# Cached cross-attention keys loaded one head at a time through two small rings, half of them during the two projections ahead of the scores

## The chip, the cores and the metric

One NeuronCore of a Trainium2 chip runs the whole program. The metric is the device time of one execution in microseconds (us), the median over runs. TensorE (PE in the profile) multiplies matrices, VectorE (DVE), ScalarE (ACT) and GpSimd (POOL) work on elements, and SyncE (SP) issues most of the transfers; 16 DMA engines carry them between the chip's memory and the on-chip buffer.

## The reference, cut to what matters

One decoder layer is computed for 256 prompt tokens and for 8 sample sequences of 4 tokens (32 sample tokens), in float32. The part that matters here is the cross-attention: the prompt tokens attend to keys and values computed from `mem_prompt`, the sample tokens to keys and values that come ready from a cache of 8 batches x 256 memory tokens x 4 heads x 512.

```python
def cross_attn(h, k, v, w_q, w_o):
    q = (h @ w_q).reshape(B, S, X_HEADS, X_HEAD_DIM)
    s = jnp.einsum('bqhd,bkhd->bhqk', q, k) * (X_HEAD_DIM ** -0.5)
    pr = jax.nn.softmax(s, axis=-1)
    o = jnp.einsum('bhqk,bkhd->bqhd', pr, v).reshape(B, S, D_MODEL)
    return o @ w_o

x = x + merged @ w_out
mk, mv = mem_kv(mem_prompt, g_mem, w_xk, w_xv)      # prompt: two more products
x = x + cross_attn(rms_norm(x, g_xattn), mk, mv, w_xq, w_xo)            # prompt
x = x + cross_attn(rms_norm(x, g_xattn), cache_mem_k, cache_mem_v, w_xq, w_xo)  # sample
```

## The kernel before, in words

All activations are held transposed (features on the 128 partitions, 288 tokens in a row). Each weight matrix is streamed in chunks of 512 rows x 512 columns (1 MB), in an order written out in `plan` (lines 121 to 143). A chunk passes through three stages: `load_w` (line 149) issues its load on SP into one of three `raw` buffers; `split_w` (line 160) makes of each half a rounded part `w_hi` on ACT (line 172) and a remainder `w_lo` on DVE (line 173), in three buffers each; `product` (lines 239 to 241) or `proj_mem` (lines 274 to 276) multiplies with three matmuls for each pair of tiles. `advance(i)` keeps the loads about three chunks and the splits two halves ahead of the half that PE is at.

Other work is put between the halves by a clock. After each half `tick()` advances it by one step (in `proj_mem` by half a step, twice a half), and runs what `later(n, fn)` put down for that step. So a step is one half of a chunk on PE. Everything is written in this order into the queue of its engine, and each engine takes its queue in order. An SP transfer that waits for a buffer therefore holds up every SP transfer behind it, the weight chunks too.

The stages around the change, one after another, have 32 steps each:

- the output projection `w_out` (in `residual`, line 828), which adds into `xT` and prepares the next operands;
- the query projection `w_xq` (loop at line 884), which writes the queries `q`. In its last quarter `mem_prompt` is loaded and transposed (lines 845 and 850);
- the memory keys `w_xk` (loop at line 1067, `proj_mem`). A quarter's result goes to memory by ACT's queue (lines 1073 and 1074). The cached keys and the sample scores are put between its steps;
- the memory values `w_xv` (loop at line 1077), with the prompt attention of one head in each quarter, and the cached values between its steps.

The cached keys of one batch are 2 MB. `k_load` (line 898) issues them as 16 transfers of 128 KB in pieces of 512 bytes, into two buffers `kv` of two heads each. `k_transposed` (line 910) transposes them on DVE, a head at a time (line 914), into `kT`, a ring of six. `k_scores` (line 920) multiplies them with `qm`, the queries of all eight batches laid out with zeros in the other batches' columns (a 128x4096 tile, cleared by POOL at line 840, filled by eight copies at line 929), and all batches are added up in one PSUM bank. A batch takes its turn every 3.8 steps of `w_xk`: load and transpose at step 1 + 3.8b, scores at 3 + 3.8b (lines 1049 to 1051). At step 31 the softmax follows (line 945), at 31.5 its transposition (line 952) with 16 DVE copies into `pTm`. The cached values come at 33 + 3.6b, a load of 1 MB and its matmuls at a time (lines 964 and 969).

Of the kernel before, what the change touches and what calls it, by code (L numbers as in the profile page):

```python
# [8 lines left out]
F32 = mybir.dt.float32  # L9
# [7 lines left out]
P = 128  # L17
DM = 2048
# [20 lines left out]
def decoder_step_kernel(  # L39
# [27 lines left out]
    def psum():  # L67
        t = ps_pool.tile([P, 512], F32, name="ps", tag="ps")
        return t
# [27 lines left out]
    def later(n, fn):  # L97
        clock[1] += 1
        pending.append((clock[0] + n, clock[1], fn))
# [728 lines left out]
    act, box = residual(w_out, act, G_XATTN)  # L828
# [5 lines left out]
    qm = xp.tile([P, KT, NB, NS], F32, name="qm", tag="qm")  # L834
# [59 lines left out]
    def split_tile(name, shape, dtype=F32):  # L894
        t = xp.tile(shape, dtype, name=name, tag="kT", bufs=6)
        return t

    def k_load(b):
        kvs = []
        for hp in range(2):  # L900
            kv = kv_tile()
            for h2 in range(2):
                for qd in range(4):
                    nc.sync.dma_start(  # L904
                        kv[32 * qd:32 * qd + 32, h2 * 1024:(h2 + 1) * 1024].rearrange("p (m r) -> p m r", r=P),
                        cache_mem_k[0, b, :, 2 * hp + h2, qd * P:(qd + 1) * P].rearrange("(m p) r -> p m r", p=32))
            kvs.append(kv)
        return kvs

    def k_transposed(kvs):  # L910
        kTs = []
        for h in range(4):
            kT = split_tile("kT", [P, 4, MEM])
            v_.transpose(kT.rearrange("p k (m c) -> p k m c", c=32),
                         kvs[h // 2][:, (h % 2) * 1024:(h % 2 + 1) * 1024].rearrange(
                             "p (m k r) -> p k m r", k=4, r=32))
            kTs.append(kT)
        return kTs

    def k_scores(kTs, b):  # L920
        for k in range(4):
            for h in range(4):
                t_.matmul(ssc[32 * h:32 * h + 32, :MEM], qm[:, 4 * h + k, b, :], kTs[h][:, k, :],
                          start=b == 0 and k == 0, stop=b == NB - 1 and k == 3, tile_position=(0, 32 * h))

    mem_transposed(3)
    mem_rstd()
    for b in range(NB):
        g_.tensor_copy(qm[:, :, b, DQ * b:DQ * b + DQ], q[:, :, NP + DQ * b:NP + DQ * b + DQ])
    ssc = psum()  # L930
# [12 lines left out]
    sbox = {}  # L943

    def sample_softmax():
        psm = t288("psm")[:, :MEM]
        softmax_rows(ssc[:, :MEM], psm, P)
        pTm = xp.tile([P, 2, NB, 4, NS], F32, name="pTm", tag="qm")
        v_.memset(pTm, 0.0)
        sbox["psm"], sbox["pTm"] = psm, pTm  # L950

    def sample_probs():
        psm, pTm = sbox["psm"], sbox["pTm"]
        pt = psum()
        for c in range(2):
            t_.transpose(pt[:, c * P:(c + 1) * P], psm[:, c * P:(c + 1) * P], ident)
        for c in range(2):
            pv = pt[:, c * P:(c + 1) * P].rearrange("p (h s) -> p h s", h=4)
            for b in range(NB):
                v_.tensor_copy(pTm[:, c, b, :, 4 * b:4 * b + 4], pv[:, :, 4 * b:4 * b + 4])  # L960
        osc = psum()
        sbox["osc"] = osc

    def v_load(c, b):
        kv = kv_tile()
        nc.sync.dma_start(kv, cache_mem_v[0, b, c * P:(c + 1) * P].rearrange("m h d -> m (h d)"))
        return kv

    def sample_values(kv, c, b):
        for h in range(4):  # L970
            t_.matmul(sbox["osc"][32 * h:32 * h + 32, :], sbox["pTm"][:, c, b, h, :], kv[:, h * 512:(h + 1) * 512],  # L971
                      start=b == 0 and c == 0, stop=b == NB - 1 and c == 1, tile_position=(0, 32 * h))

    def sample_out():
        os_sb = small.tile([P, 512], F32, name="os_sb", tag="kn", bufs=3)
# [13 lines left out]
    def head_load(h):  # L989
        kn = wpool.tile([P, 4, 512], F32, name="knat", tag="raw")  # L990
        for qd in range(4):
            nc.sync.dma_start(kn[32 * qd:32 * qd + 32, :2].rearrange("p t (m r) -> p (t m) r", r=P),
                              k_scr[:, h * 512 + qd * P:h * 512 + (qd + 1) * P].rearrange("(m p) r -> p m r", p=32))
        k_hi = split_tile("k_hi", [P, 4, MEM], F32R)
        k_lo = split_tile("k_lo", [P, 4, MEM], F32R)
        q_hi = split_tile("q_hi", [P, 4, NP], F32R)
        q_lo = split_tile("q_lo", [P, 4, NP], F32R)
# [21 lines left out]
    def head_probs():  # L1019
        pr = hb["pr"]  # L1020
        pt = psum()
        for c in range(2):
            for i in range(2):
                t_.transpose(pt[:, c * 256 + i * P:c * 256 + (i + 1) * P], pr[:, i, c * P:(c + 1) * P], ident)
        p_hi = xp.tile([P, 2, NP], F32R, name="p_hi")
        p_lo = xp.tile([P, 2, NP], F32R, name="p_lo")
        split_act(p_hi, p_lo, pt.rearrange("p (c t) -> p c t", c=2))
        hb["p"] = (p_hi, p_lo)

# [10 lines left out]
    kts = {}  # L1040

    def k_unit(b):
        kts[b] = k_transposed(k_load(b))

    def v_unit(b):
        for c in range(2):
            sample_values(v_load(c, b), c, b)
# [7 lines left out]
    later(60, sample_out)  # L1055
    later(60.5, sample_out2)

    act = Quarters()

# [17 lines left out]
    for h in range(4):  # L1077
        later(1, lambda h=h: head_load(h))
        later(3, lambda h=h: head_keys(h, 0))
        later(3, lambda h=h: head_keys(h, 2))  # L1080
        later(4, lambda: head_scores(0))
        later(5, lambda: head_scores(1))
        later(7, head_probs)
        v_hi = xp.tile([P, 2, 512], F32R, name="v_hi")
        v_lo = xp.tile([P, 2, 512], F32R, name="v_lo")
# [135 lines left out]
```

## Time and profile before

| | |
|---|---|
| median of 3 runs | 2201.93 us (2196.97, 2201.93, 2201.97) |
| the profiled execution's own time | 2195.65 us |
| its span, first to last instruction | 2193.9 us |
| mean granted TensorE clock | 0.995 of 2.4 GHz |
| busy share PE / PEld / DVE / ACT / POOL | 98% / 94% / 59% / 39% / 1% |
| moved by DMA | 397.50 MB, mean 181 GB/s |

The page cuts the span into 40 slices of 54.8 us; its PE row shows where TensorE is less than fully busy, its DMA row how busy the 16 DMA engines are. A busy share is an average over a slice, so the stage where it dips is then read in finer stretches, by its waits and by what SP issues.

### The profile page before, as it was taken

Reading aid. Unit: us, or ns where it says so; the run is one execution under the profiler, and the core shown is the slowest. Engines: PE = TensorE matmul, PEld = TensorE weight load, DVE = VectorE, ACT = ScalarE, POOL = GpSimd, SP = SyncE. Lnnn points to the kernel's source line nnn. Section 1 sums busy time; section 2 is a strip of 40 time slices with the busy share of each in tenths; the row PEclk is TensorE's granted clock in tenths of the full one; section 3 lists DMA queues with packets and bytes.
Section 4 is the critical chain, followed back from the end, with each engine's and each line's share of the span. In section 5 each row is a group of like instructions: output and inputs, shape, how many; then the busy total and the mean of one; then the engine's idle time right before and its main releaser. Section 6 shows DMA issues by size and latency. Waiting matters only on the chain.

```text
span 2193.9 us, 36832 instructions
## 1 busy us (share of the span) xinstructions
PE 2147.2 (98%) x15559; PEld 2059.9 (94%) x15559; DVE 1289.0 (59%) x1972; ACT 863.6 (39%) x1188; POOL 25.3 (1%) x70
## 2 busy tenths in 40 slices
PE   8999999999999999998789999999999999999998
PEld 7999999999999999996457799999999999999998
DVE  7667877677475656455555656554455445445554
ACT  6444433343344435352134445333333333333343
POOL 1000000000000000000000000000000000000000
PEclk9999999999999999999999999999999999999999
DMA  7546445444545554569998745454554555555542
GB/s 252 190 158 203 149 152 171 162 165 155 175 164 192 185 163 165 163 182 262 264 287 291 252 161 172 156 173 160 167 171 158 171 165 162 173 160 167 171 156 101
DMA packets 221113, 397.50 MB, mean 181 GB/s; under 512 B 9146, under 2 KB 47674, under 8 KB 218491
## 3 DMA queue, kind: packets, MB, share of 16 engines
q1 hardware_dynamic: 215813, 384.36, 55.1%
q10 hardware_dynamic: 4878, 10.72, 1.4%
q8 instruction: 122, 2.00, 0.4%
q14 instruction: 44, 0.36, 0.0%
q0 software_dynamic: 256, 0.05, 0.0%
HBM read 383.51 MB, written 12.80 MB: 181 GB/s over the span
## 4 chain that ended last, share of the span: by engine, by line
PE 54%; issue 38%; DMA 5%; DVE 1%; SPq 1%; ACT 0%; ACTq 0%; POOL 0%; POOLq 0%; DVEq 0%
PE ps L239 15%; PE ps L241 15%; PE ps L240 15%; DMA kv<-in_cache_mem_k_dram 2%; DMA raw<-in_w_xk_dram 2%; PE ps L275 2%; PE ps L274 2%; PE ps L276 2%; PE ps L971 1%; DMA k_scr<-kn 1%; DVE w_lo L173 0%; DMA raw<-in_w_in_dram 0%; SPq L904 0%; PE ps L647 0%; DMA out_dram<-kn 0%
## 5 line engine op out<-in xcount | busy, mean ns | idle before, releaser
L173 DVE TENSOR_TENSOR w_lo<-raw,w_hi 128x1024 fp32r<-128x1024 f32 (+1 forms) x673 | 784.8, 1171 | 815.0 <-ACT w_hi L172 812.1
L172 ACT CAST w_hi<-raw 128x1024 fp32r<-128x1024 f32 (+1 forms) x673 | 672.9, 1006 | 1185.2 <-PE ps L240 959.4
L239 PE MATMUL ps<-q_hi,w_hi 128*128 128x288 f32 x3200 | 947.0, 296 | 1.4 <-ACT w_hi L172 0.7
L241 PE MATMUL ps<-q_hi,w_lo 128*128 128x288 f32 x3200 | 943.6, 295 | 1.2 <-DVE w_lo L173 1.2
L240 PE MATMUL ps<-q_lo,w_hi 128*128 128x288 f32 x3200 | 943.4, 295 | 0.7 <-DVE q_lo L200 0.7
L239 PEld LDWEIGHTS ps<-q_hi,w_hi 128*128 128x128 f32 x3200 | 601.0, 188 | 2.9 <-ACT w_hi L172 0.9
L240 PEld LDWEIGHTS ps<-q_lo,w_hi 128*128 128x128 f32 x3200 | 601.2, 188 | 1.5 <-DVE q_lo L200 0.9
L241 PEld LDWEIGHTS ps<-q_hi,w_lo 128*128 128x128 f32 x3200 | 600.5, 188 | 1.6 <-DVE w_lo L173 1.6
L241 PE MATMUL ps<-h_hi,w_lo 128*128 128x288 f32 x1024 | 302.2, 295 | 0.0
L239 PE MATMUL ps<-h_hi,w_hi 128*128 128x288 f32 x1024 | 301.9, 295 | 0.0
L240 PE MATMUL ps<-h_lo,w_hi 128*128 128x288 f32 x1024 | 301.5, 294 | 0.0
L239 PEld LDWEIGHTS ps<-h_hi,w_hi 128*128 128x128 f32 x1024 | 192.1, 188 | 0.0
L240 PEld LDWEIGHTS ps<-h_lo,w_hi 128*128 128x128 f32 x1024 | 192.1, 188 | 0.0
L241 PEld LDWEIGHTS ps<-h_hi,w_lo 128*128 128x128 f32 x1024 | 192.1, 188 | 0.0
L241 PE MATMUL ps<-y_hi,w_lo 128*128 128x288 f32 x384 | 113.3, 295 | 0.0
L240 PE MATMUL ps<-y_lo,w_hi 128*128 128x288 f32 x384 | 113.1, 294 | 0.0
L239 PE MATMUL ps<-y_hi,w_hi 128*128 128x288 f32 x384 | 113.0, 294 | 0.0
L275 PE MATMUL ps<-w_lo,q_hi 128*128 128x512 f32 x256 | 102.8, 401 | 3.1 <-DVE w_lo L173 3.1
L527 DVE SCALAR_TENSOR_TENSOR cv<-glu,cwT,cv 128x256 f32<-128x256 f32 x240 | 105.7, 477 | 0.0
L274 PE MATMUL ps<-w_hi,q_hi 128*128 128x512 f32 x256 | 101.9, 404 | 1.7 <-ACT w_hi L172 1.7
L276 PE MATMUL ps<-w_hi,q_lo 128*128 128x512 f32 x256 | 101.1, 395 | 0.0
L239 PEld LDWEIGHTS ps<-y_hi,w_hi 128*128 128x128 f32 x384 | 72.0, 188 | 0.0
(300 smaller groups left out, 1266.8 us busy)
## 6 DMA issues: line engine op xcount, KB each, us to landing
raw<-in_w_in_dram SPq DMA_DIRECT2D x87, 1024.0 KB
raw<-in_w_up_dram SPq DMA_DIRECT2D x64, 1024.0 KB
raw<-in_w_down_dram SPq DMA_DIRECT2D x64, 1024.0 KB
raw<-in_w_branch_dram SPq DMA_DIRECT2D x24, 1024.0 KB
raw<-in_w_out_dram SPq DMA_DIRECT2D x16, 1024.0 KB
raw<-in_w_xq_dram SPq DMA_DIRECT2D x16, 1024.0 KB
raw<-in_w_xk_dram SPq DMA_DIRECT2D x16, 1024.0 KB
kv<-in_cache_mem_k_dram SPq DMA_DIRECT2D x128, 128.0 KB
```

What stands on the lines that cost most here:

```text
L172: latest["hi"] = s_.copy(dh, src)
L173: latest["lo"] = v_.tensor_tensor(dl, src, dh.bitcast(F32), ALU.subtract)
L239: t_.matmul(o, wh, act.hi(kt), start=kt == 0, stop=False)
L240: t_.matmul(o, wh, act.lo(kt), start=False, stop=False)
L241: t_.matmul(o, wl, act.hi(kt), start=False, stop=kt == nkt - 1)
L274: t_.matmul(acc[c], mh, hi[:, i, :], start=kt == 0, stop=False)
L275: t_.matmul(acc[c], mh, lo[:, i, :], start=False, stop=False)
L276: t_.matmul(acc[c], ml, hi[:, i, :], start=False, stop=kt == KT - 1)
L527: v_.scalar_tensor_tensor(o, i, wk, o, ALU.mult, ALU.add)
L971: t_.matmul(sbox["osc"][32 * h:32 * h + 32, :], sbox["pTm"][:, c, b, h, :], kv[:, h * 512:(h + 1) * 512], start=b == 0 and c == 0, stop=b ...
```

## The change

- `xattn`'s buffers are opened ahead of `w_out` instead of behind it. `base` is the clock at the first step of `w_xk`, and `at(step, fn)` counts from there; `w_out` and `w_xq` are the steps -64 to 0.
- Keys are loaded and transposed a head at a time (32 pieces of 512 KB, in four transfers of 128 KB as before), through six `kv` buffers of one head and a ring of nine `kT`. Heads 0 to 14 are issued at steps -62, -58, ... -6, heads 0 to 8 transposed at -60, -56, ... -28. Head n from 9 on is transposed at 1.5 + 2.5((n - 9) // 4) + 0.3((n - 9) mod 4), and head n from 15 on is issued 0.2 behind the transposition of head n - 6.
- Scores of batch b at 1 + 2.5b, its masked queries half a step before: POOL clears a 128x512 tile and copies one batch's columns.
- Softmax at 20, its transposition at 21, with one ACT copy to `psT`; the masked probabilities are built per batch by POOL (a clear and a copy).
- Values of batch b at 24 + 5b; their loads are pieces of 512 KB (two heads) through the same six `kv` buffers.
- The split keys, queries, probabilities and values of the prompt attention use the ring of nine too.

```diff
+    xa = ExitStack()            # (ahead of residual(w_out, ...) now)
+    base = clock[0] + 64
+    def at(step, fn):
+        later(base + step - clock[0], fn)
+    def ring_tile(name, shape, dtype=F32):
+        t = xp.tile(shape, dtype, name=name, tag="ring", bufs=9)
     def kv_tile():
-        kv = xp.tile([P, DM], F32, name="kv", bufs=2)
+        kv = xp.tile([P, 1024], F32, name="kv", bufs=6)
-    later(2, lambda: g_.memset(qm, 0.0))
+    def k_load(n):
+        b, h = divmod(n, 4)
+        kv = kv_tile()
+        for qd in range(4):
+            nc.sync.dma_start(
+                kv[32 * qd:32 * qd + 32].rearrange("p (m r) -> p m r", r=P),
+                cache_mem_k[0, b, :, h, qd * P:(qd + 1) * P].rearrange("(m p) r -> p m r", p=32))
+        kraw[n] = kv
+    def q_masked(b):
+        qm = xp.tile([P, KT, NS], F32, name="qm", bufs=2)
+        g_.memset(qm, 0.0)
+        g_.tensor_copy(qm[:, :, DQ * b:DQ * b + DQ], q[:, :, NP + DQ * b:NP + DQ * b + DQ])
+    def score_step(b):
+        return 1 + 2.5 * b
+    def value_step(b):
+        return 24 + 5 * b
+    def k_step(n):
+        if n < 9:
+            return 4 * n - 60
+        return score_step((n - 9) // 4) + 0.5 + 0.3 * ((n - 9) % 4)
+    for n in range(32):
+        at(4 * n - 62 if n < 15 else k_step(n - 6) + 0.2, lambda n=n: k_load(n))
+        at(k_step(n), lambda n=n: k_transposed(n))
+    for b in range(NB):
+        at(score_step(b) - 0.5, lambda b=b: q_masked(b))
+        at(score_step(b), lambda b=b: k_scores(b))
+    act, box = residual(w_out, act, G_XATTN)
...
-        pTm = xp.tile([P, 2, NB, 4, NS], F32, name="pTm", tag="qm")
-        v_.memset(pTm, 0.0)
...
-                v_.tensor_copy(pTm[:, c, b, :, 4 * b:4 * b + 4], pv[:, :, 4 * b:4 * b + 4])
+        s_.copy(psT, pt[:, :MEM].rearrange("p (c h s) -> p c h s", c=2, h=4))
+    def probs_masked(b):
+        pTm = xp.tile([P, 2, 4, NS], F32, name="pTm", bufs=2)
+        g_.memset(pTm, 0.0)
+        g_.tensor_copy(pTm[:, :, :, bs], sbox["psT"][:, :, :, bs])
...
-        later(1 + 3.8 * b, lambda b=b: k_unit(b))
-        later(3 + 3.8 * b, lambda b=b: k_scores(kts.pop(b), b))
-        later(33 + 3.6 * b, lambda b=b: v_unit(b))
-    later(31, sample_softmax)
-    later(31.5, sample_probs)
+    at(20, sample_softmax)
+    at(21, sample_probs)
+        at(value_step(b) - 0.5, lambda b=b: probs_masked(b))
+        at(value_step(b), lambda b=b: sample_values(b))
+    for n in range(32):
+        at(k_step(26 + n) + 0.2 if n < 6 else value_step((n - 6) // 4) + 0.5 + (n - 6) % 4, lambda n=n: v_load(n))
```

## Rows read from the trace of the kernel before

**Rows 1.** The page, part 2: busy tenths, clock and DMA in 40 slices.
```profile
PE   8999999999999999998789999999999999999998
...
DMA  7546445444545554569998745454554555555542
GB/s 252 190 158 203 149 152 171 162 165 155 175 164 192 185 163 165 163 182 262 264 287 291 252 161 172 156 173 160 167 171 158 171 165 162 173 160 167 171 156 101
```
**Rows 2.** Stretches: length, busy time (instructions) by engine, clock, DMA share, GB/s.
```profile
760.00:960.00 200.00, 200.00 (x1511) 199.62 (x1510) 108.91 (x175) 85.67 (x141) 5.82 (x3) 1.00 0.50 165
973.00:1124.00 151.00, 123.92 (x646) 81.82 (x644) 87.49 (x84) 36.89 (x43) 2.87 (x9) 0.97 1.07 266
1131.00:1139.00 8.00, 8.00 (x36) 6.61 (x37) 4.19 (x6) 3.43 (x5) 0.00 (x0) 1.00 0.47 137
1121.50:1128.30 6.80, 4.53 (x12) 3.68 (x13) 3.57 (x20) 1.42 (x3) 0.00 (x0) 0.50 0.91 300
1140.00:1240.00 100.00, 100.00 (x544) 74.42 (x544) 56.14 (x83) 44.03 (x70) 0.00 (x0) 1.00 0.85 303
```
**Rows 3.** Waits from 950 to 1250 us: total, times, longest.
```profile
ACT w_hi L172 <- DMA raw<-in_w_xk_dram: 91.4, 14, 13.2
...
PEld ps L923 <- DVE kT L914: 23.4, 15, 2.7
DVE kT L914 <- DMA kv<-in_cache_mem_k_dram: 20.3, 15, 2.5
...
PE ps L956 <- DVE psm L941: 5.4, 1, 5.4
```
**Rows 4.** Timeline of PE at the edges of the w_xk stage, and one score batch.
```profile
973.21 0.48 PE L274 MATMUL ps<-w_hi,q_hi 128*128 128x512 f32 x1
...
1124.11 0.78 PE L274 MATMUL ps<-w_hi,q_hi 128*128 128x512 f32 x1
...
992.09 1.68 PE L923 MATMUL ps<-kT,qm 128*32 128x256 f32 x24
993.70 0.50 PE L274 MATMUL ps<-w_hi,q_hi 128*128 128x512 f32 x1
...
1129.00 1.92 PE L971 MATMUL ps<-kv,pTm 128*32 128x512 f32 x16
```
**Rows 5.** Transfers of 970 to 1107 us; last, key issues (ns, first, last).
```profile
DMA packets 43323, 34.75 MB, mean 254 GB/s; under 512 B 2423, under 2 KB 34398, under 8 KB 43315
...
q1 hardware_dynamic: 41587, 31.50, 100.0%
...
kv<-in_cache_mem_k_dram SPq DMA_DIRECT2D x128, 128.0 KB
raw<-in_w_xk_dram SPq DMA_DIRECT2D x14, 1024.0 KB
k_scr<-kn ACTq DMA_DIRECT2D x6, 256.0 KB
out_dram<-kn ACTq DMA_DIRECT2D x6, 256.0 KB
...
L904 SPq DMA_DIRECT2D kv<-in_cache_mem_k_dram x128: 311/442/1970, 970.4 to 1106.0; - x128
```
**Rows 6.** Splits and transpositions, 950 to 1260 us: busy, mean ns, idle before.
```profile
L173 DVE TENSOR_TENSOR w_lo<-raw,w_hi 128x1024 fp32r<-128x1024 f32 x66 | 79.9, 1223 | 85.9 <-ACT w_hi L172 85.8
L172 ACT CAST w_hi<-raw 128x1024 fp32r<-128x1024 f32 x68 | 70.5, 1049 | 169.3 <-DMA raw<-in_w_xk_dram 91.4 <-PE ps L276 49.2 <-issue 13.7
...
L914 DVE STREAM_TRANSPOSE kT<-kv 128x1024 f32<-128x1024 f32 x32 | 39.2, 1236 | 21.7 <-DMA kv<-in_cache_mem_k_dram 20.3 <-issue 1.3
```
**Rows 7.** POOL's timeline around the masked queries: start, us, instruction.
```profile
768.21 3.52 POOL L840 MEMSET qm<- 128x4096 f32 x1 [134.26 <-issue]
...
972.86 2.31 POOL L929 COPY qm<-q 128x64 f32<-128x64 f32 x8 [100.47 <-DVE q L886]
975.83 0.70 POOL L283 TENSOR_TENSOR r_mem<-ms,mhalf 128x2 f32<-128x2 f32 x1 [0.66 <-DVE ms L869]
```
**Rows 8.** SP's w_out loads, and DVE's evacuations of w_out and w_xo.
```profile
743.82 95.27 SPq L154 DMA_DIRECT2D raw<-in_w_out_dram  x16
...
L818 DVE TENSOR_TENSOR xT<-xT,ps x32: 446/449/455, 787.7 to 1361.1; 128x288 f32<-128x288 f32 x32
```

More of the change, by code (lines that the diff above doesn't have):

```diff
@@ L826, in residual @@
         return new, box
-    act, box = residual(w_out, act, G_XATTN)
     xa = ExitStack()
@@ L833, in decoder_step_kernel, with k_transposed, k_scores @@
     q = xp.tile([P, KT, NT], F32, name="q")
-    qm = xp.tile([P, KT, NB, NS], F32, name="qm", tag="qm")
+    base = clock[0] + 64
[3 more added lines that the diff above has]
+        t = xp.tile(shape, dtype, name=name, tag="ring", bufs=9)
+        return t
     def kv_tile():
-        kv = xp.tile([P, DM], F32, name="kv", bufs=2)
+        kv = xp.tile([P, 1024], F32, name="kv", bufs=6)
         return kv
-    later(2, lambda: g_.memset(qm, 0.0))
+    kraw, kts = {}, {}
+    def k_load(n):
[6 more added lines that the diff above has]
+        kraw[n] = kv
+    def k_transposed(n):
+        kT = ring_tile("kT", [P, 4, MEM])
+        v_.transpose(kT.rearrange("p k (m c) -> p k m c", c=32),
+                     kraw.pop(n).rearrange("p (m k r) -> p k m r", k=4, r=32))
+        kts[n] = kT
+    def q_masked(b):
+        qm = xp.tile([P, KT, NS], F32, name="qm", bufs=2)
+        g_.memset(qm, 0.0)
+        g_.tensor_copy(qm[:, :, DQ * b:DQ * b + DQ], q[:, :, NP + DQ * b:NP + DQ * b + DQ])
+        sbox["q", b] = qm
+    def k_scores(b):
+        qm = sbox.pop(("q", b))
+        kT = [kts.pop(4 * b + h) for h in range(4)]
+        for k in range(4):
+            for h in range(4):
+                t_.matmul(sbox["sc"][32 * h:32 * h + 32, :MEM], qm[:, 4 * h + k, :], kT[h][:, k, :],
+                          start=b == 0 and k == 0, stop=b == NB - 1 and k == 3, tile_position=(0, 32 * h))
+    sbox = {}
+    def score_step(b):
[13 more added lines that the diff above has]
+    act, box = residual(w_out, act, G_XATTN)
     m1 = Quarters(MEM)
@@ L892, in decoder_step_kernel @@
         proj(w_xq, KT, h * 512, act, evac_q)
[L894 to L924, printed above, removed]
     mem_transposed(3)
     mem_rstd()
-    for b in range(NB):
-        g_.tensor_copy(qm[:, :, b, DQ * b:DQ * b + DQ], q[:, :, NP + DQ * b:NP + DQ * b + DQ])
-    ssc = psum()
+    assert clock[0] == base
+    sbox["sc"] = psum()
     def softmax_rows(sc, out, rows):
@@ L956, in sample_probs, with v_load, sample_values @@
             t_.transpose(pt[:, c * P:(c + 1) * P], psm[:, c * P:(c + 1) * P], ident)
-        for c in range(2):
-            pv = pt[:, c * P:(c + 1) * P].rearrange("p (h s) -> p h s", h=4)
-            for b in range(NB):
-                v_.tensor_copy(pTm[:, c, b, :, 4 * b:4 * b + 4], pv[:, :, 4 * b:4 * b + 4])
[L961 to L972, printed above, removed]
+        psT = xp.tile([P, 2, 4, NS], F32, name="psT")
+        s_.copy(psT, pt[:, :MEM].rearrange("p (c h s) -> p c h s", c=2, h=4))
+        osc = psum()
+        sbox["psT"], sbox["osc"] = psT, osc
+    def probs_masked(b):
+        pTm = xp.tile([P, 2, 4, NS], F32, name="pTm", bufs=2)
+        g_.memset(pTm, 0.0)
+        bs = slice(DQ * b, DQ * b + DQ)
+        g_.tensor_copy(pTm[:, :, :, bs], sbox["psT"][:, :, :, bs])
+        sbox["p", b] = pTm
+    vraw = {}
+    def v_load(n):
+        b, c, hp = n // 4, n // 2 % 2, n % 2
+        kv = kv_tile()
+        nc.sync.dma_start(kv.rearrange("p (h d) -> p h d", h=2),
+                          cache_mem_v[0, b, c * P:(c + 1) * P, 2 * hp:2 * hp + 2])
+        vraw[n] = kv
+    def sample_values(b):
+        pTm = sbox.pop(("p", b))
+        for c in range(2):
+            for h in range(4):
+                t_.matmul(sbox["osc"][32 * h:32 * h + 32, :], pTm[:, c, h, :],
+                          vraw[4 * b + 2 * c + h // 2][:, (h % 2) * 512:(h % 2 + 1) * 512],
+                          start=b == 0 and c == 0, stop=b == NB - 1 and c == 1, tile_position=(0, 32 * h))
     def sample_out():
@@ L1024, in head_probs @@
                 t_.transpose(pt[:, c * 256 + i * P:c * 256 + (i + 1) * P], pr[:, i, c * P:(c + 1) * P], ident)
-        p_hi = xp.tile([P, 2, NP], F32R, name="p_hi")
-        p_lo = xp.tile([P, 2, NP], F32R, name="p_lo")
+        p_hl = ring_tile("p_hl", [P, 2, 2, NP], F32R)
+        p_hi, p_lo = p_hl[:, 0], p_hl[:, 1]
         split_act(p_hi, p_lo, pt.rearrange("p (c t) -> p c t", c=2))
@@ L1038, in head_values @@
         s_.copy(q[:, 4 * h + d, :NP], po[:, :NP])
[L1040 to L1047, printed above, removed]
-    for b in range(NB):
-        later(1 + 3.8 * b, lambda b=b: k_unit(b))
-        later(3 + 3.8 * b, lambda b=b: k_scores(kts.pop(b), b))
-        later(33 + 3.6 * b, lambda b=b: v_unit(b))
-    later(31, sample_softmax)
-    later(31.5, sample_probs)
-    later(60, sample_out)
-    later(60.5, sample_out2)
+    at(20, sample_softmax)
+    at(21, sample_probs)
+    for b in range(NB):
+        at(value_step(b) - 0.5, lambda b=b: probs_masked(b))
+        at(value_step(b), lambda b=b: sample_values(b))
+    for n in range(32):
+        at(k_step(26 + n) + 0.2 if n < 6 else value_step((n - 6) // 4) + 0.5 + (n - 6) % 4, lambda n=n: v_load(n))
+    at(60, sample_out)
+    at(60.5, sample_out2)
     act = Quarters()
@@ L1083, in decoder_step_kernel @@
         later(7, head_probs)
-        v_hi = xp.tile([P, 2, 512], F32R, name="v_hi")
-        v_lo = xp.tile([P, 2, 512], F32R, name="v_lo")
+        v_hi = ring_tile("v_hi", [P, 2, 512], F32R)
+        v_lo = ring_tile("v_lo", [P, 2, 512], F32R)
         def evac_v2(c, acc, h=h, v_hi=v_hi, v_lo=v_lo):
```

15 lines of the change are left out of this document (7 added, 8 removed).

## The prediction, made before the change was run

> **What bounds the kernel now.** I read the page's slices first. TensorE is fully busy nearly everywhere; it dips in one place, the four slices where the DMA row stands at 9, 9, 8 and the GB/s are highest without being best [rows 1]. The stretches say which stage that is: from 760 to 960 us, in `w_out` and `w_xq`, PE is busy 200 of 200 us and the DMA engines half; from 973 to 1124 us, in `w_xk`, PE is busy 123.92 of 151 us and the DMA share is 1.07, so saturated; in `w_xv` PE is busy all the time again [rows 2]. The waits name the late thing: the splits of `w_xk` waited 91.4 us for their chunk (14 times), the key transpositions 20.3 us for keys, PE 23.4 us for transpositions [rows 3]. So one stage is bound by its transfers, and its neighbours have half of the DMA engines to spare.
>
> How much is lost there: the stage lasts from 973.21 to 1124.11, 150.9 us [rows 4]. Its own matmuls run at 8.00 us for 36 where nothing disturbs them [rows 2], 0.222 us each; 12 make a step, 2.67 us, and 32 steps 85.4 us. A score batch is 32 matmuls; 24 of them took 1.61 us until the next one began [rows 4], so 2.1 us a batch, 16.8 in all; the softmax's two transpositions 0.7. That is 102.9 us; **48.0 us is waiting**, and no edit of this change can win much more than that.
>
> **The change part by part.** *What a transfer costs where DMA is the bound.* In 760 to 960 us a share of 0.50 moved 165 GB/s [rows 2], so a megabyte takes 3.03 us of all 16 engines, a weight chunk 3.18. Between the first key issue at 970.4 and the last at 1106.0 lie 135.6 us [rows 5], filled by 32 heads of keys, 14 chunks (44.5) and 12 results of 256 KB (9.5): 81.6 us are left for keys, **2.55 us a head**. The bounds: 2.85 if the results went beside the rest for nothing, 1.47 if a head cost what as many bytes cost in `w_xv`, where the values are read in long pieces (share 0.85 at 303 GB/s [rows 2]). The first rows measure the keys themselves, so I take 2.55.
>
> *15 of 32 heads go early.* 15 x 2.55 = 38 us of transfers leave the saturated stage for two stages that last 203 us and whose engines are idle half the time; their share becomes about 0.69. What covers them: a step there is 24 x 200/1511 = 3.18 us, the first evacuation at 787.7 lies 8 steps behind the start, so `w_out` starts at 762.3, and its first chunk was issued at 743.8 [rows 8], 18.5 us earlier; its split comes two steps ahead of use, which leaves 12 us. A chunk alone takes some 2 us to start and 3.18; with a head ahead of it in SP's queue 2.55 more, 8 us in all. I cost them at nothing; a head issues four transfers of 0.44 us [rows 5], 1.8 us of SP, inside the same 12 us. Head 0 waits until the branch stage's buffers are free: POOL's clear of `qm`, in the same pool, could run at 768.21 [rows 7], 6 us into `w_out`; the fourth chunk of `w_out` stands behind it and lands some 2 + 2.55 + 3.18 us later, 13.6 us into the stage; its split is due at step 4, 12.7 us, but its matmuls only at step 6, 19 us, so PE doesn't notice. The nine early transpositions of 1.24 us [rows 6] fall where DVE is busy 108.91 of 200 us [rows 2], and each comes two steps behind its load in the order of the code, more in time since SP runs ahead: nothing.
>
> *The 17 heads left.* They are not spread over the stage: all are written into SP's queue between steps 2 and 12, four a score batch, with only every second step a chunk between them, and every chunk of `w_xk` stands behind them. So I follow the queue, in us from 973.2. Scores of batch 0 come at step 1 but need their masked queries: POOL does `r_mem` first, until 976.5, then clears an eighth of 3.52 us and copies 0.29 [rows 7], so they are ready at 4.0 where PE arrives at 2.7: **1.3 us** of new wait, once (later batches have half a step, 1.3 us, for 0.7). They end at 6.1, head 9 is transposed at 7.4, frees its buffer, and head 15 can be issued; chunk 3 waits behind heads 15 and 16. From here, with 2 us until data flow, the transfers are one row. With heads at 2.55, chunks at 3.18, half-value loads at 1.47 and 3.2 for a quarter's results behind steps 8 and 16, chunks 4 to 8 land at 26.0, 39.3, 55.9, 66.7 and 76.5, chunk 10 at 93.4. A chunk is usable 2.3 us later (1.05 and 1.22 for the first half's splits [rows 6]). PE, at 5.34 us for a chunk's two steps and 2.1 a score batch, comes to chunk 5 at 36.4 and waits 5.2, to chunk 6 after 7.5 more and waits 9.1, to chunk 7 and waits 3.4, to chunk 8 and waits 4.4; then head 31 has landed, the queue holds only chunks and values, and PE is the bound again but for 2.0 at chunk 10. The scores themselves wait for nothing more: head 31 lands near 72, PE is at step 18.5 near 88. Together with the 1.3: 25.4 us.
>
> *Softmax and values.* The softmax moves to step 20, its transposition a step later, 2.67 us; DVE's big clear and 16 copies become one ACT copy and POOL's small clears, off the path. PE's wait of 5.4 there [rows 3] can stay whole or vanish; the step covers half of it and DVE's clear is gone: I take 1. Behind that wait the clock stood at 0.50 until 1128.3 [rows 2], of which 4.2 us fell into `w_xv`, a loss of 2.1; that I count as gone. Two value batches move from `w_xv` to steps 24 and 29 (16 matmuls, 1.92 us a batch [rows 4]): the same work on PE in either place. Their loads wait for the batch before on PE, with a weight chunk behind them; that chunk is needed four steps later, 10.7 us, against 2 + 2 x 1.47 + 3.18 = 8.1: nothing, with little room.
>
> **The sum.** Waits of 48.0 become 26.4, a win of 21.6; with the clock's 2.1, 23.7 us. The profiled execution's 2195.65 us becomes 2172.0. The runs shown have a mean 4.6 us above it (their median 6.3), so I state 2177 for the median of the new one.
>
> Beside this stands the clock. What the rows show is one stretch at 1.2 GHz behind a wait of 5.4 us, while the mean over the stage is 0.97 for all its many waits of 1 to 3 us [rows 2, 3]. The Trainium skill (TensorE: Matmul & The Clock Gate, HAM oscillation) says that a kernel whose bursts of matmuls alternate with waits for DMA starts each burst cold; this speaks against a change that turns many short waits into four longer ones. By it the sum would lose 2.1 us for each of the two longest, 19.5 instead of 23.7. I leave it at 23.7, because a slower burst ahead of the next late chunk only shortens the wait for that.
>
> **The rivals.** *Cheap keys.* If a head cost 1.47 us, as its bytes do in long pieces, the same queue gives 7 us of waits, and the win is 41 and 2 more: 2152.6 by the profile, 2157 for the median. For it: with 15 heads fewer in flight, packets overlap less. Against: the keys' packets are 512 bytes (34398 of 43323 are under 2 KB) and the queue was 100.0% busy at a mean of 254 GB/s [rows 5], where `w_xv` moved 303 at 0.85. The Trainium skill (DMA: Bandwidth & Descriptors, Specifications) gives 512 bytes as enough for line rate; by that this rival would be the forecast, and the trace does not bear it out.
>
> *Slower: weights late in the two early stages.* There PE has no slack at all, so a late chunk is paid in full. The place is each of the 15 chunks that stand behind an early head in SP's queue; the price, if they are as late as `w_xk`'s, is 91.4/14 = 6.5 us each, 98 in all, less the 23.7: 2275 for the median. From 1.6 us each on it eats the whole win; at 2 us each the time is 2207, slower than before. It decides when a chunk takes over 12 us instead of 8. Against it is the half-empty DMA row there [rows 1, 2].
>
> *Nothing comes early.* If the six `kv` buffers or the ring came free only late in `w_xq`, all 32 heads would again meet in `w_xk`, 48 us of waiting would stay, and the time with it: 2200. Against it: the space was free at 768.21 [rows 7].
>
> **How the numbers follow.** The forecast, a stage still held up by its keys in its first half, has 0.70; within it a win of 12 to 34 us (heads at 2.85 cost 5 more, a softmax wait kept whole 4, the clock 4; heads at 2.3 win 4, no late results 6), 2166 to 2188. Cheap keys have 0.17, nothing early 0.07, slower 0.06. The range reaches from cheap keys to the weak end of the forecast: 2157 to 2190. A measurement of this kernel can tell 0.3% from no change, 6.6 us; so faster takes the first two, 0.87, the same 0.07, slower 0.06.
>
> **What would show it.** In the changed profile: keys issued from about 765 us on; the DMA share of 760 to 960 us near 0.69 with PE still busy throughout; `w_xk` some 20 us shorter; splits waiting for chunks 5 to 8 by 3 to 9 us and hardly after; PE hardly waiting for transpositions. Wrong would be a `w_out` or `w_xq` that grows (slower rival), a `w_xk` with no waits for chunks (cheap keys), or one that waits for chunks in its second half too, which would mean that something else than keys fills the queue.

## The result, and the profile of the changed kernel

The changed kernel takes **2168.68 us** (median of 4 runs, 2167.57 to 2173.44) against 2199.94 us for the kernel before in the same comparison (4 runs, 2196.97 to 2201.97): a ratio of **0.9863, 95% interval 0.9842 to 0.9884**. Its profiled execution took 2167.95 us, with a span of 2166.1 us, 27.8 us shorter than before.

I read it in the order of the prediction. First the page's part 2, to be laid beside [rows 1]:

```profile
PE   8999999999999999998899999999999999999998
...
DMA  7546444544545577769998554545554555455542
GB/s 248 192 150 212 159 156 156 168 164 158 174 157 174 201 216 206 203 195 233 284 335 278 178 167 157 174 158 174 157 174 157 174 158 173 159 172 160 172 156 103
```

The dip of PE has shrunk from three slices to two, and the DMA row now rises from the fifteenth slice on (7, 7, 7, 6 where 5, 4, 5, 6 stood): the early heads. The same stretches as in [rows 2], as far as they answer to them (length, busy time and instructions of PE, PEld, DVE, ACT and POOL, granted clock, DMA share, GB/s):

```profile
760.00:960.00 200.00, 200.00 (x1509) 199.48 (x1509) 118.88 (x184) 85.62 (x141) 3.78 (x6) 1.00 0.72 204
...
973.00:1050.00 77.00, 66.38 (x431) 45.86 (x432) 47.13 (x48) 18.34 (x24) 6.91 (x15) 0.93 1.05 251
1050.00:1110.00 60.00, 57.00 (x275) 42.27 (x274) 28.14 (x29) 21.01 (x22) 1.40 (x6) 0.97 0.90 316
...
1027.00:1033.00 6.00, 3.82 (x8) 2.62 (x9) 3.88 (x4) 1.99 (x2) 0.00 (x0) 0.50 1.23 205
...
985.00:1001.00 16.00, 16.00 (x118) 11.52 (x117) 11.12 (x11) 4.80 (x5) 1.53 (x4) 1.00 1.18 204
```

In `w_out` and `w_xq` PE is busy 200 of 200 us as before, at a DMA share of 0.72 for 0.50. The first 77 us of `w_xk` lack 10.6 us of PE, the next 60 lack 3.0. The last line is a stretch in which SP issues nothing but keys: the DMA engines are full, yet move only 204 GB/s; this line becomes the key to the rest. Now PE's timeline at the first matmul of chunks 0, 5, 6, 7, 8, 10 and 11 of `w_xk` and of `w_xv`, with some of the score matmuls between them (start, length, instruction, idle time before it and what ended it), to be laid beside [rows 4]:

```profile
973.90 0.48 PE L274 MATMUL ps<-w_hi,q_hi 128*128 128x512 f32 x1
...
976.84 1.93 PE L874 MATMUL ps<-kT,qm 128*32 128x256 f32 x32
...
1009.67 2.35 PE L874 MATMUL ps<-kT,qm 128*32 128x256 f32 x34
1011.94 0.73 PE L274 MATMUL ps<-w_hi,q_hi 128*128 128x512 f32 x2
...
1029.14 1.22 PE L274 MATMUL ps<-w_hi,q_hi 128*128 128x512 f32 x2 [7.35 <-ACT w_hi L172]
...
1037.05 0.63 PE L874 MATMUL ps<-kT,qm 128*32 128x256 f32 x4
1039.73 0.50 PE L274 MATMUL ps<-w_hi,q_hi 128*128 128x512 f32 x1 [2.06 <-ACT w_hi L172]
...
1047.47 1.93 PE L874 MATMUL ps<-kT,qm 128*32 128x256 f32 x30
1049.33 0.73 PE L274 MATMUL ps<-w_hi,q_hi 128*128 128x512 f32 x2
...
1065.35 0.73 PE L274 MATMUL ps<-w_hi,q_hi 128*128 128x512 f32 x2 [1.99 <-ACT w_hi L172]
...
1073.56 0.40 PE L274 MATMUL ps<-w_hi,q_hi 128*128 128x512 f32 x1
...
1105.03 0.39 PE L274 MATMUL ps<-w_hi,q_hi 128*128 128x512 f32 x1
```

So `w_xk` lasts from 973.90 to 1105.03, **131.1 us where 150.9 stood**; it begins 0.7 us later than before. `w_xv` lasts until 1228.1 (the first matmul of `w_xo`), **123.0 us for 131.8**; everything behind it takes 938.1 us in both traces. That is -19.8, -8.7 and +0.7: the whole 27.8 us.

The waits from 950 to 1250 us (total, times, longest), for [rows 3]:

```profile
ACT w_hi L172 <- DMA raw<-in_w_xk_dram: 51.0, 6, 14.3
PEld ps L274 <- ACT w_hi L172: 16.9, 9, 7.8
...
PE ps L274 <- ACT w_hi L172: 11.4, 3, 7.3
...
DVE kT L859 <- DMA kv<-in_cache_mem_k_dram: 2.5, 1, 2.5
```

The chunks are late six times instead of 14, for 51.0 us of ACT's time instead of 91.4, and keys hold up a transposition once, for 2.5 us, instead of 20.3. (The same answer puts four more waits of these splits, 8.2 us in all, down to transfers that they don't read; they may be late chunks too.) And SP's queue in the stretch that is still held up (start, length, transfers in a row):

```profile
979.28 0.37 SPq L154 DMA_DIRECT2D raw<-in_w_xk_dram  x1
980.43 21.83 SPq L852 DMA_DIRECT2D kv<-in_cache_mem_k_dram  x32
1002.37 0.40 SPq L154 DMA_DIRECT2D raw<-in_w_xk_dram  x1
1004.34 16.55 SPq L852 DMA_DIRECT2D kv<-in_cache_mem_k_dram  x16
1020.99 0.40 SPq L154 DMA_DIRECT2D raw<-in_w_xk_dram  x1
1021.48 9.26 SPq L852 DMA_DIRECT2D kv<-in_cache_mem_k_dram  x12
1031.09 0.39 SPq L154 DMA_DIRECT2D raw<-in_w_xk_dram  x1
```

Eight heads (32 transfers) stand between two chunks; they take 21.83 us, **2.73 us a head**. Behind them the heads take more of SP's time, 16.55 us for four and 9.26 for three; there chunks, results and waits for buffers lie between them. Chunk 5, issued behind them at 1002.37, reaches PE at 1011.94, and chunk 6, behind four more heads, is the one that PE waits 7.35 us for.

### The profile page after: what moved, and what is told of

It reads as the page before. It is cut to its first block, busy times and chain, and to the rows that moved or that the text cites. A ratio compares the mean times of both kernels' runs of the same rounds, so it can differ in the third digit from the quotient of the medians.

```text
span 2166.1 us, 36855 instructions
## 1 busy us (share of the span) xinstructions
PE 2132.5 (98%) x15559; PEld 2060.2 (95%) x15559; DVE 1284.6 (59%) x1955; ACT 865.1 (40%) x1189; POOL 31.3 (1%) x93
## 4 chain that ended last, share of the span: by engine, by line
PE 56%; issue 38%; DMA 4%; DVE 1%; SPq 1%; ACT 0%; POOL 0%; ACTq 0%; POOLq 0%; DVEq 0%
PE ps L241 15%; PE ps L239 15%; PE ps L240 15%; PE ps L274 2%; PE ps L275 2%; PE ps L276 2%; DMA kv<-in_cache_mem_k_dram 1%; DMA raw<-in_w_xk_dram 1%; PE ps L1003 1%; SPq L852 0%; DMA raw<-in_w_in_dram 0%; DVE w_lo L173 0%; PE ps L647 0%; ACT w_hi L172 0%; DMA k_scr<-kn 0%
## 5 line engine op out<-in xcount | busy, mean ns | idle before, releaser
L274 PEld LDWEIGHTS ps<-w_hi,q_hi 128*128 128x128 f32 x256 | 48.6, 192 | 29.3 <-ACT w_hi L172 16.9
```

Source lines behind the costliest of these rows:

```text
L274: t_.matmul(acc[c], mh, hi[:, i, :], start=kt == 0, stop=False)
```

## The experiments

The theory was the prediction's: the gain comes from the 15 early heads alone; the 17 that are left fill SP's queue at some 2.6 us each, and the chunks stand behind them. Its open point is what makes a head cost that. In the diffs `...` stands for lines left out. All kernels are edits of the changed one; the ratio is always to the kernel before, run on the same chip, so 0.9863 is the value to beat. Stage lengths are read as above.

**e1: nothing early.** Every head goes into `w_xk`, and scores, softmax and values return to the steps of before; head-wise loads, rings and per-batch masks stay.

```diff
-        at(4 * n - 62 if n < 15 else k_step(n - 6) + 0.2, lambda n=n: k_load(n))
+        at(0.5 if n < 6 else k_step(n - 6) + 0.2, lambda n=n: k_load(n))
...
-        return 1 + 2.5 * b
+        return 3 + 3.8 * b
...
```

> The changed kernel with its rings of one head and its masked tiles per batch, but no head of keys ahead of w_xk: loads, transpositions, scores, softmax and values at the steps of the kernel before. Queue theory (w_xk is held up by what its transfers cost, so the gain is the 15 heads that leave the stage): all 32 heads meet in w_xk again, its 151 us come back, 2193 to 2203 us. Rival (the smaller rings and tiles are worth something by themselves): 2175 to 2188 us.

Measured 2195.64 us, ratio 0.9988 (0.9979 to 0.9998), as the queue theory expected: the gain is gone but for 0.1%. `w_xk` takes 155.9 us, `w_xv` 126.6. Smaller pieces, rings and masks are worth about nothing by themselves; coming early is what pays. PE's timeline at the end of `w_xk` shows what became of the softmax's wait of 5.4 us [rows 3]; at the old step it is 1.37 us:

```profile
1129.22 0.44 PE L975 MATMUL ps<-ident,psm 128*128 128x128 f32 x2 [1.37 <-DVE psm L964]
1129.41 0.48 PE L274 MATMUL ps<-w_hi,q_hi 128*128 128x512 f32 x1
```

**e5: nine heads early, not fifteen.** Heads 9 to 14 are issued at the start of `w_xk`; nothing else differs.

```diff
-        at(4 * n - 62 if n < 15 else k_step(n - 6) + 0.2, lambda n=n: k_load(n))
+        at(4 * n - 62 if n < 9 else 0.5 if n < 15 else k_step(n - 6) + 0.2, lambda n=n: k_load(n))
```

> The changed kernel with 9 instead of 15 heads early; heads 9 to 14 are issued at step 0.5 of w_xk. Queue theory: six more heads are 15.3 us more of transfers in the stage; the engines are idle for its first 5 to 7 us, which takes two or three of them, so the time is 8 to 12 us more, 2176 to 2181 us. Rival (only the first heads matter, those that the scores wait for first): 2167 to 2171 us.

Measured 2187.22 us, ratio 0.9951 (0.9934 to 0.9968), 18.5 us above the changed kernel and 6 beyond what I expected; `w_xk` takes 150.0 us, 18.9 more. So six heads cost 3.1 us each, more than I allowed. SP's timeline gives the same price (26 transfers are 6.5 heads):

```profile
975.09 20.17 SPq L852 DMA_DIRECT2D kv<-in_cache_mem_k_dram  x26
```

That is 3.10 us a head. The stage grew by as much as six heads take of SP's queue, so no part of a head looks hidden. The two sizes aren't the same thing, though: the mean granted clock of the stage also fell, from 0.95 to 0.89, and its share of the 18.9 us wasn't taken apart.

**e7: the early heads in a bunch.** Heads 0 to 14 are issued at steps -17 to -3 instead of -62 to -6, and heads 0 to 8 transposed at -15 to -7.

```diff
-            return 4 * n - 60
+            return n - 15
...
-        at(4 * n - 62 if n < 15 else k_step(n - 6) + 0.2, lambda n=n: k_load(n))
+        at(n - 17 if n < 15 else k_step(n - 6) + 0.2, lambda n=n: k_load(n))
```

> The changed kernel with the 15 early heads issued one a step in the last 17 steps of w_xq instead of one every four steps over w_out and w_xq. What makes the early heads free is, by my account, that each chunk there has some 4 us to spare. A step of 3.18 us then has 2.55 + 1.59 us of transfers, 4.14 us: over 15 steps 14 us too many, less what is in hand, so w_xq grows by 6 to 12 us and the time is 2174 to 2181 us. Rival (PE never notices a transfer there): 2166 to 2171 us.

Measured 2185.82 us, ratio 0.9945 (0.9929 to 0.9962), 5 us above the range that I expected. `w_xk` starts at 989.6, some 16 us late, and then takes 135.4 us. The stretches in the second half of `w_xq` of this kernel (columns as above):

```profile
920.00:940.00 20.00, 20.00 (x153) 20.00 (x153) 14.54 (x20) 7.15 (x13) 0.00 (x0) 1.00 1.10 235
940.00:960.00 20.00, 17.99 (x124) 17.76 (x124) 12.32 (x19) 6.07 (x12) 0.00 (x0) 0.91 1.10 240
960.00:980.00 20.00, 17.61 (x132) 16.91 (x130) 7.60 (x15) 8.19 (x20) 0.00 (x0) 1.00 1.09 233
```

This is the mechanism of the slower rival, seen at work: with the DMA share at 1.10 the loads of a stage without slack come late. From 900 to 990 us the splits wait 8.1 us for chunks of `w_xq`, and PE waits once, 4.7 us, for `mem_prompt`, whose loads stand behind the same heads. It is real, and a head every fourth step is thin enough to avoid it.

**e2: softmax and values late.** The softmax back at step 31, the values at 33 + 3.6b; the early keys stay.

```diff
-        return 24 + 5 * b
+        return 33 + 3.6 * b
...
-    at(20, sample_softmax)
-    at(21, sample_probs)
+    at(31, sample_softmax)
+    at(31.5, sample_probs)
...
```

> The changed kernel with softmax and values at the steps of the kernel before (31, 31.5, 33 + 3.6b). If moving them is only moving (my account: the same work on PE in either stage, and one wait of some 5 us with its slow clock back at the end of w_xk): 2170 to 2176 us, w_xk 4 us shorter by the two value batches and w_xv 4 us longer, plus up to 5 + 2 us for the softmax. If the early values also relieve w_xv's transfers: 2174 to 2180 us.

Measured 2168.81 us, ratio 0.9866 (0.9848 to 0.9884): no difference, and below both ranges that I expected. `w_xk` becomes 5.1 us shorter and `w_xv` 4.3 longer. Moving the softmax and two value batches moves work and wins nothing; the softmax's wait, which I expected back with some 5 us, is 1.46 us at the old step.

**e4: the remaining heads spread out.** Heads 15 to 31 are issued 1.4 steps apart, score batches 3.8 apart, softmax and values late.

```diff
-        return 1 + 2.5 * b
+        return 1 + 3.8 * b
...
-        at(4 * n - 62 if n < 15 else k_step(n - 6) + 0.2, lambda n=n: k_load(n))
+        at(4 * n - 62 if n < 15 else max(k_step(n - 6) + 0.2, 1.7 + 1.4 * (n - 15)), lambda n=n: k_load(n))
...
```

> The changed kernel with the 17 heads that are left issued one every 1.4 steps up to step 24 (instead of four at a time up to step 12), scores every 3.8 steps, softmax at 29, values from 33. Queue theory: the weight chunks no longer stand behind four heads each; waits of 24 us become about 10, spread out, and the time is 2153 to 2159 us. Rival (the transfers of the stage as a whole are the bound, however ordered): 2165 to 2170 us. If the last scores become late instead: over 2172 us.

Measured 2170.53 us, ratio 0.9881 (0.9866 to 0.9896): the time is near the rival's, but not for its reason. `w_xk` falls by 13.6 us to 117.5. e2, with its softmax and values as late, has 126.0 there, so spreading the keys saves 8.5 us of it. But `w_xv` rises from 123.0 to 140.8. e2 has the same eight value batches in `w_xv` and needs 127.3, so 13.5 us are new. The groups of PE's instructions in `w_xv` have them: the 128 value matmuls (busy, mean ns, idle before), first in e2, then in e4:

```profile
L1003 PE MATMUL ps<-kv,pTm 128*32 128x512 f32 x128 | 15.4, 598 | 0.0
```
```profile
L1006 PE MATMUL ps<-kv,pTm 128*32 128x512 f32 x128 | 27.6, 602 | 0.0
```

The same matmuls occupy PE for 12.2 us more, because they come in shorter runs: e2 has whole batches of 16 in 1.92 us, e4 mostly runs of 2 to 8 of some 1.05 us each, with other matmuls between them. And SP's own waits in e4 from 1085 to 1240 us show its queue standing at their loads (line 998 here):

```profile
SPq L998 <- PE ps L1006: 45.0, 10, 10.2
```

The keys that were spread left the first value loads to the end of `w_xk` (1077 to 1082 us, where e2 has them from 1040 to 1053), and the later ones wait for the batch before. That this is why the batches come apart is argued; no run shows it. The gain was given back one stage later.

**e3: long pieces.** Each transfer still brings 128 KB to 32 partitions, but in pieces of 2048 bytes instead of 512. Here, and in e10 and e11, the keys lie in another order, so the sample scores are of wrongly paired features; all instructions behind the loads are the same.

```diff
-                kv[32 * qd:32 * qd + 32].rearrange("p (m r) -> p m r", r=P),
-                cache_mem_k[0, b, :, h, qd * P:(qd + 1) * P].rearrange("(m p) r -> p m r", p=32))
+                kv[32 * qd:32 * qd + 32].rearrange("p (m r) -> p m r", r=512),
+                cache_mem_k[0, b, 64 * qd:64 * qd + 64, h, :].rearrange("(m p) r -> p m r", p=32))
```

> The changed kernel, with the same bytes of a head of keys read in pieces of 2048 bytes instead of 512 (the keys then lie in another order, so the scores are of other numbers). Queue theory: a head costs about 1.6 us instead of 2.55, the waits for chunks 5 to 8 shrink from some 24 to 7 to 10 us, w_xk from 131 to 114 to 118 us, 2152 to 2157 us. Rival (the waits come from the order of rings, transpositions and scores, not from what a head costs): 2166 to 2171 us.

Measured 2172.81 us, ratio 0.9893 (0.9876 to 0.9909): no gain at all; my expectation fell, and `w_xk`, at 133.9 us, is even 2.8 longer. Eight heads still take 19.97 us of SP's queue, 2.50 each, and the stretch of keys alone reads

```profile
985.00:1001.00 16.00, 16.00 (x118) 11.73 (x118) 11.12 (x10) 4.21 (x4) 1.53 (x4) 1.00 1.00 230
```

230 GB/s for 204: four times longer pieces bring an eighth. The length of a piece is at most a small part of what a head costs. Two ideas were left. *W*: a transfer that writes only 32 of the 128 partitions is slow. *F*: SP keeps only eight transfers in flight (by their semaphores, each waits for the transfer eight before it). SP's waits of the changed kernel from 973 to 1060 us:

```profile
SPq L852 <- DMA kv<-in_cache_mem_k_dram: 13.1, 26, 4.0
```

**e10: wide.** The same four transfers of 128 KB from the same addresses in pieces of 512 bytes, but each to all 128 partitions.

```diff
-                kv[32 * qd:32 * qd + 32].rearrange("p (m r) -> p m r", r=P),
-                cache_mem_k[0, b, :, h, qd * P:(qd + 1) * P].rearrange("(m p) r -> p m r", p=32))
+                kv[:, 256 * qd:256 * qd + 256].rearrange("p (m r) -> p m r", r=P),
+                cache_mem_k[0, b, :, h, qd * P:(qd + 1) * P].rearrange("(m p) r -> p m r", p=P))
```

> The changed kernel with each of a head's four transfers of 128 KB written to all 128 partitions instead of to 32 (same pieces of 512 bytes, same number and size of transfers; the keys then lie in another order, so the scores are of other numbers). Two theories for what makes a head cost 2.6 us though not its pieces. Theory W (a transfer to 32 partitions is slow, because all 16 engines then write into the same quarter of the buffer): a head costs about 1.5 us, w_xk 114 to 118 us instead of 131, 2151 to 2157 us. Theory F (eight transfers of 128 KB in flight, each 5 us long, are the bound): unchanged, 2165 to 2171 us.

Measured **2155.56 us, ratio 0.9803** (0.9787 to 0.9819); `w_xk` takes 119.0 us. The time is in theory W's range, `w_xk` 1 us above it. The stretch of keys alone in this kernel:

```profile
985.00:991.00 6.00, 6.00 (x51) 4.11 (x50) 4.37 (x5) 1.43 (x2) 0.77 (x2) 1.00 1.10 278
```

It ends at 991 here, since SP issues a chunk at 991.56; the changed kernel has 205 GB/s in the same 6 us. So 278 GB/s with pieces as short as before, and SP's timeline has five heads at 2.25 us each (the next seven, behind that chunk, 2.69):

```profile
980.22 11.24 SPq L852 DMA_DIRECT2D kv<-in_cache_mem_k_dram  x20
```

So F is not the cause: the number of transfers and their size are the changed kernel's. W stands, though a head came down to 2.25 us and not to 1.5. One thing isn't told apart from it: with the partitions, the order in which a transfer's pieces are read from memory changes too.

**e11: one transfer a head.** 512 KB to all 128 partitions, in pieces of 2048 bytes.

```diff
-        for qd in range(4):
...
+        nc.sync.dma_start(
+            kv.rearrange("p (m r) -> p m r", r=512),
+            cache_mem_k[0, b, :, h, :].rearrange("(m p) r -> p m r", p=P))
```

> The changed kernel with a head of keys in one transfer of 512 KB to all 128 partitions, in pieces of 2048 bytes (another order of the keys again). Both theories, W and F, expect a head of about 1.5 us, w_xk 112 to 118 us and 2150 to 2157 us; together with the run on four wide transfers it tells them apart. If neither holds (the heads' rows in the chip's memory are the bound): 2165 to 2171 us.

Measured **2149.05 us, ratio 0.9774** (0.9759 to 0.9788); `w_xk` takes 112.1 us, 5.4 above the 106.7 that its matmuls need. The split's wait for chunks and, by SP's waits from 981 to 1012 us, what holds SP now:

```profile
ACT w_hi L172 <- DMA raw<-in_w_xk_dram: 23.5, 5, 7.4
...
SPq L851 <- DVE kT L858: 19.3, 13, 3.4
```

With quick transfers SP hardly waits for landings any more, but for DVE to give the six buffers back. e11 takes away 19.0 of the 24.4 us of waiting that the changed kernel still had, e10 12.1 of them. Both theories expected e11, which came out 1 us below their range; it is e10 that tells them apart.

**e12 and e13: a second queue.** Two of each head's four transfers are issued from POOL (e12) or from ACT (e13), in the original order.

```diff
-            nc.sync.dma_start(
+            (nc.sync if qd % 2 == 0 else g_).dma_start(
```

> The changed kernel with two of a head's four transfers issued by POOL instead of SP, nothing else. Under W two quarters of the buffer are written at once for longer, under F twice as many transfers are in flight: both expect a head nearer to 1.6 us and 2152 to 2162 us. If POOL's queue is slow or its waits hold up the masked queries: 2168 to 2180 us.

> As the run before, with ACT's queue instead of POOL's. The same gain, 2152 to 2162 us, unless ACT, which takes its queue in order, stands waiting for a buffer with the splits of the weights behind it: then 2170 us and more.

Measured 2164.18 us, ratio 0.9841 (0.9827 to 0.9856), for POOL and 2165.60, ratio 0.9850 (0.9833 to 0.9867), for ACT. `w_xk` gets 5.3 and 3.9 us shorter; e13's starts 2.4 us later, but so does its `w_out` (at 766.14 for 763.52), ahead of every key. The intervals overlap with the changed kernel's, so whether either is faster at all stays open. Both theories expected more, 2162 us at the most. A second queue takes at most 5.3 us from `w_xk`, where e11 takes 19.0.

**e14 and e15: wide in the right order.** A head as eight transfers of 64 KB, each bringing 32 positions to all 128 partitions, so that the keys lie as the scores need them; half from POOL (e14), or all from SP (e15).

```diff
-        for qd in range(4):
...
+        for m in range(8):
+            (nc.sync if m % 2 == 0 else g_).dma_start(
+                kv[:, P * m:P * m + P],
+                cache_mem_k[0, b, 32 * m:32 * m + 32, h, :].rearrange("p (q r) -> q p r", q=4))
```

> Each head comes as eight transfers of 64 KB, one for each group of 32 cached positions, each written to all 128 partitions in pieces of 512 bytes, in the key order of the changed kernel; four are issued from SP and four from POOL. Theory W (the price of a head is set by how many partitions one transfer writes): the heads in w_xk cost near those of e10_wide (2.25 us), the stretch is near its 119 us, and with the eight smaller issues dearer the time is 2154 to 2163 us. Rival (the issues or the smaller transfers are the price: twice as many issues as in the changed kernel, and each queue keeps fewer bytes in flight): no better than e12_two_queues, 2164 or more, and the weights' conversion still waits some 50 us in w_xk.

> The same eight transfers of a head, all from SP. Theory W with the queue's eight in flight: eight transfers are now 512 KB in flight and not 1 MB, and eight issues of about 0.4 us are 3.2 us for a head, more than the 2.7 us of the changed kernel, so that the gain of writing wide is lost in the issues: 2164 to 2176 us, w_xk 127 to 139 us. Rival (an issue costs nothing once the transfers drain faster): as e14_rows_two_queues, under 2163.

Measured 2207.32 us, ratio 1.0043 (1.0029 to 1.0056), and 2229.14 us, ratio 1.0147 (1.0133 to 1.0161): both slower than the kernel before. e14 lies on its rival's side (its splits wait 59.2 us for chunks in `w_xk`), e15 outside both expectations. The stretch of keys alone in e15, its issues (ns shortest/median/longest, first and last start), and its SP timeline:

```profile
990.00:1010.00 20.00, 18.34 (x127) 12.99 (x125) 8.24 (x7) 4.21 (x4) 1.53 (x4) 1.00 0.29 84
```
```profile
L852 SPq DMA_DIRECT2D kv<-in_cache_mem_k_dram x256: 521/722/3404, 769.8 to 1099.9; - x128
```
```profile
981.47 29.07 SPq L852 DMA_DIRECT2D kv<-in_cache_mem_k_dram  x37
```

The DMA engines are idle seven tenths of the time at 84 GB/s, while SP issues one transfer after another at 0.79 us each: 6.3 us a head. This is not the cost of an ordinary issue: its median is 0.72 us here, 0.45 in the changed kernel for twice the bytes. Such a share is what four or five of the 16 engines make if they alone have the work. The Trainium skill (DMA: Bandwidth & Descriptors, Why a DMA increments its semaphore by 16 and not by 1) says that the number of engines for a transfer is the largest up to 16 that divides the slowest dimension of both access patterns; the source of these is written with the four feature groups outermost, so four engines by that rule, a quarter of 16. The share of 0.29 agrees with that; no run here has the same transfers with another outermost dimension. If that is the reason, e14 and e15 say nothing against W; it remains argued. A quick load in the right order has not been found.

## Why the prediction was right, point by point

**The sum.** The profiled executions differ by 27.7 us where 23.7 was forecast, 4.0 more: `w_xk` has 2.0 us less of waiting than forecast and `w_xv` won 2.8 more, while `w_xk` began 0.7 later. The median came out 8.3 us below 2177; the other 4.3 are the step from profile to median, which I set at 4.6 and rounded up, and which is 0.7 for these runs. The weak end of the forecast's own range was added up wrongly (5, 4 and 4 off 23.7 leave 10.7 us and not 12); the measured win lies far above either.

**The queue.** Waits of 48.0 us in `w_xk` were to become 26.4. Measured: 131.1 less the 102.9 of its own work and 3.8 for two value batches leaves **24.4**. The queue ran as I had followed it: I had chunks 5, 6, 7, 8 and 10 land 16.6, 10.8, 9.8 and 16.9 us apart, and they start on PE 17.2, 10.6, 9.6 and 16.0 us apart. The single waits I had less well. They are read from the starts above and chunk 9's at 1055.68, with 5.34 us for two steps and 2.1 for every 32 score matmuls that the trace has between. PE went to chunk 5 without a wait (5.2 forecast): chunks 3 and 4 were issued by 979.28, ahead of the first of these heads, where I had them behind some, and a score batch that I had behind the chunk's first half ran ahead of it, at 1009.67. Chunk 6 came 9.8 us late (9.1), chunk 7 5.0 (3.4), chunk 8 2.3 (4.4), as nearly the whole score batch lies between 7 and 8, chunk 9 1.0 (0), chunk 10 2.5 (2.0) and chunk 11, behind the softmax, 2.2 (1 for the softmax). The errors have both signs, so that their sum is only 2.0 us off is in part luck.

**The price of a head** was right in size and wrong in cause. I took 2.55 us between 1.47 and 2.85; SP's queue shows 2.73 for the first eight, six heads less in e5 3.1, and the early ones raise the share from 0.50 to 0.72, 44 us for 15 heads or 2.9 each (I had forecast 0.69). But what I argued from, that short packets fill the DMA engines, fell with e3; e10 comes down to 2.25 with pieces just as short. What costs, by e10, is that a transfer writes only 32 partitions (or the order of reading that goes with it). The Trainium skill (SBUF — State Buffer, Door 1: The DMA port swizzle) states the rule that I should have weighed: a transfer's rate goes by how many of the 16 ports its partitions reach, and partitions 0 to 31 reach eight. The traces agree with it, with 204 and 230 GB/s to 32 partitions and 278 GB/s to 128, though they don't show ports. The 512 bytes that the prediction cited from the Trainium skill are no contradiction either, since e10 runs at 278 GB/s with such pieces. *Cheap keys* was thus a possible kernel, but not this one.

**The masked queries** were a term of the sum that failed outright. I charged 1.3 us because POOL would do `r_mem` first; score batch 0 ran at 976.84 without a wait. POOL's timeline shows why:

```profile
768.55 0.99 POOL L865 MEMSET qm<- 128x512 f32 x2 [134.27 <-issue]
...
973.36 1.25 POOL L866 COPY qm<-q 128x64 f32<-128x64 f32 x2 [99.73 <-DVE q L944]
976.37 0.70 POOL L283 TENSOR_TENSOR r_mem<-ms,mhalf 128x2 f32<-128x2 f32 x1 [1.76 <-DVE ms L927]
```

The first two clears ran 200 us early, since their tiles were free, and the copies come ahead of `r_mem`. Copies ahead of `r_mem` stood in [rows 7] already; I read them in the wrong order.

**Early heads at no cost** held: PE is busy 200 of 200 us, `w_out` and `w_xq` take as long as before to 0.4 us, and head 0 went out behind POOL's clear at 768.58. That this has a limit is shown by e7.

**`w_xv`** was to win 5.9 us and won 8.7. e1, with the softmax at its old step and all eight value batches in the stage, takes 126.6 us there, 5.2 less than before; the two batches that move make the other 3.5 (forecast 3.8). Of the 5.2, the slow clock of [rows 2] was to be 2.1; 3.1 more I had not counted. But e1's `w_xk` is 5.0 us longer than before, so that part of the gain in `w_xv` is no gain by itself, as e2 shows too.

**The clock.** Behind the wait of 7.35 us the granted clock was 0.50 from 1027 to 1033, so chunk 6's matmuls began slowly. The rule that the prediction took from the Trainium skill (TensorE: Matmul & The Clock Gate, HAM oscillation), that a burst behind a wait for DMA starts cold, agrees with that. The clock stood at 0.50 twice more in this stage, in chunk 7 behind a wait of 2.06 us and in chunk 10 behind one of 1.99:

```profile
1040.30:1043.60 3.30, 2.81 (x7) 2.13 (x7) 3.30 (x4) 0.33 (x1) 0.00 (x0) 0.50 1.11 285
...
1067.60:1070.90 3.30, 3.30 (x9) 2.54 (x9) 2.15 (x6) 1.91 (x4) 0.00 (x0) 0.50 0.64 200
```

The kernel before, too, had two such stretches in `w_xk` besides the one that I read (0.50 from 1063.5 to 1066.8 and from 1114.7 to 1118.0). That a slow burst only shortens the next wait fits the first one, since PE still waited 2.06 us for chunk 7 behind it; it remains argued, as no run took the slow clock away. Behind the last one no wait for a chunk followed that could have hidden it, some 1.7 us by my estimate (half of its 3.3 us) that the sum didn't have.

**The rivals.** *Nothing early* is e1, 2195.64 us against the 2200 given. *Slower* didn't happen, and e7 shows its mechanism at 16 us for 15 heads in a bunch, about 1 us a head.

## What to carry to other kernels

When one stage is bound by its transfers and the stages ahead have DMA time to spare, count the megabytes that can move and spread them as thinly as their consumer's slack allows: fifteen heads at every fourth step cost nothing, the same fifteen in a bunch cost 16 us. Before moving a load, look at its rate in a stretch where it runs alone: engines that are full at 204 GB/s while other transfers reach 300 say that the shape of the transfer, here the number of partitions that it writes, can be a second lever. And read the change over all stages: in e2 and e4 a stage won 5 and 14 us and the next one gave nearly all of it back, or more.

## What was unexpected of the hardware

- A transfer to 32 partitions runs at 204 GB/s with 512-byte and 230 GB/s with 2048-byte pieces, one to 128 partitions at 278 GB/s with 512-byte pieces, while the share of busy DMA engines is 1.00 to 1.18 in all three. A full share therefore doesn't mean full rate.
- Eight transfers of 64 KB whose source has four groups outermost took 6.3 us of SP's queue for a head, at a DMA share of 0.29, against 2.73 us for the same bytes in four transfers.
- SP's transfers wait for one another without any dependence of data: by their semaphores, each key transfer waits for the landing of the eighth before it (13.1 us in 26 places between 973 and 1060 us), but that is not the limit: e10 has as many in flight and reaches 278 GB/s.
